# A matmul with a decayed running sum: what TensorE runs ahead of its first product

## The chip, the core and the metric

The kernel runs on one core of a Trainium2 chip. A core has a matrix engine (TensorE, PE in the profile, with its weight loads as PEld), three engines for elementwise work (VectorE or DVE, ScalarE or ACT, GpSimd or POOL), and SyncE (SP), which here only issues DMAs. Each engine has its own instruction queue, and they meet through semaphores. Work in on-chip memory lies in SBUF; products are written to PSUM. The metric is device time in microseconds, lower is better.

## The reference

```python
B, S, D = (16, 2048, 1024)          # x: B,S,D fp32; w: D,D; decay: D
xw = x @ w
out[:, 0, :] = xw[:, 0, :]
for t in range(1, S):
    out[:, t, :] = decay[None, :] * out[:, t - 1, :] + xw[:, t, :]
```

A matrix product of 32768 rows by 1024 by 1024, and along the 2048 time steps of each batch a first-order recurrence per column.

## The kernel before

Time is cut into 64 chunks of 512 steps, and two chunks make a group. The 1024 columns of the output are cut into 8 blocks of 128, whose columns stand on the partitions of PSUM, so that the recurrence runs along the free dimension. For a block and a chunk, TensorE sums over 8 slices `k` of 128 inputs: `wsb[:, k, n]` is the stationary operand, 512 time steps of the transposed x the moving one (`matmul`, L125 to L137, all recorded at L131). Both are bf16. The whole kernel is 4096 such products, some of them cut into smaller pieces at the start and the end.

Around them: GpSimd issues the loads of x (`load`, L105), one per quarter of the partitions, with the cast to bf16; VectorE transposes 32 by 32 blocks (`turn`, L115); ScalarE and VectorE sort even and odd inputs apart (`part`, L123) into `xt`. The products' first half takes `xw` as it is, the other `xt`. The recurrence runs on VectorE, either straight (L229) or in pairs of steps with help of ScalarE and GpSimd (L171, L191, L205, L210, L266); VectorE transposes back (L278), and SP issues the stores (L302). Weights come in through `load_w` (L319): one quarter of them, in four DMAs, on the queues of SP and ScalarE, the rest on GpSimd's; `settle` (L326) casts and sorts them into `wsb`.

The order on each engine is written out by hand: every instruction passes through `pin`, which keeps it in program order on its engine. `agenda` lists deeds by letter for each step; entry -99 is the start-up: `M` loads half a chunk, `U` a quarter of the weights, `w` and `W` settle weights on ScalarE and VectorE, `E` turns, `F` and `G` sort on VectorE and ScalarE, `K3` is `spin_on(3)`.

What the change touches is ahead of that. The zeroed tile `wide` (512 fp32 columns; `idle` is its bf16 view of 512 columns) and the zeroed `seed` feed five fp32 matmuls into a PSUM tile `spare` that nobody reads (`spin(5, seed, wide)`, L347, recorded at L345). They wait for the memsets and for a one-element copy on ScalarE (L338). Then `spin_on(3)` lets ScalarE copy one column of the fourth quarter of the first half chunk of x into `gate` (L361), and one bf16 matmul of `gate` with `idle` (L345) follows it; it too is not read. The first real product comes next.

Of the kernel before, what the change touches and what calls it, by code (L numbers as in the profile page):

```python
# [9 lines left out]
FP32 = mybir.dt.float32  # L10
BF16 = mybir.dt.bfloat16
# [3 lines left out]
def _ap(ap_obj: bass.AP, new_ap, extra_offset=0):  # L15
    return dataclasses.replace(
        ap_obj,
        ap=[list(p) for p in new_ap],
        offset=ap_obj.offset + extra_offset,
    )  # L20
# [5 lines left out]
def kernel(  # L26
# [26 lines left out]
    nc = tc.nc  # L53
    pin = tc.keep_in_program_order
# [15 lines left out]
    const = ctx.enter_context(tc.tile_pool(name="const", bufs=1))  # L70
# [5 lines left out]
    def ring(pool, name, count, shape, dtype=FP32):  # L76
        i = turns[name] = turns.get(name, -1) + 1
        return pool.tile(shape, dtype, name=f"{name}{i % count}")
# [238 lines left out]
    def load_w(queues, h, e):  # L317
        for i, q in enumerate((0, 2, 1, 3)):
            pin(queues[i % len(queues)].dma_start(  # L319
                out=stage[h, e][quad(q)].rearrange("p (m d) -> p m d", m=M),  # L320
                in_=_ap(w, [[2 * D, P], [2 * P * D, M], [1, CH]],
                        (q * CQ + e) * D + h * CH)))
# [6 lines left out]
    wide = const.tile([128, TL], FP32, name="wide")  # L329
    idle = wide[:, 0:TL // 2].bitcast(BF16)  # L330
    spare = ring(psp, "spare", 1, [128, TL])
    rows = const.tile([128, 2, P], FP32, name="rows")
    seed = const.tile([128, 128], FP32, name="seed")
    load_w((nc.sync, nc.scalar), 0, 0)
    pin(nc.vector.memset(wide, 0.0))
    pin(nc.vector.memset(rows, 0.0))
    pin(nc.vector.memset(seed, 0.0))
    pin(nc.scalar.copy(out=seed[:, 0:1], in_=wide[:, 0:1]))  # L338

    gate = const.tile([128, 128], BF16, name="gate")  # L340
    pin(nc.vector.memset(gate, 0.0))

    def spin(count, by, on):
        for _ in range(count):
            pin(nc.tensor.matmul(out=spare, lhsT=by, rhs=on, start=True, stop=True))  # L345

    spin(5, seed, wide)  # L347
    H = NJ // 2
    cuts = (((0, H + 2), (H + 2, NJ)), ((0, H), (H, NJ)))
    for q in range(NQ):  # L350
        pin(nc.sync.dma_start(
            out=rows[q * P:q * P + R],
            in_=_ap(decay, [[P, R], [CH, 2], [1, P]], q * CR)))
# [399 lines left out]
```

## Time and profile before

| | |
|---|---|
| time, median of 3 runs | 903.42 us (903.32 to 903.68) |
| time of the profiled execution | 903.94 us |
| span of the profile (first to last instruction) | 902.1 us |
| busy: PE, DVE, ACT, POOL | 889.2, 826.0, 685.2, 656.7 us |
| mean granted TensorE clock | 0.999 |
| first fp32 spin starts | 3.21 us |
| bf16 spin starts | 10.32 us |
| first product starts (L131) | 10.68 us |

The profile shows one execution. Times in it count from the span's start. A group of instructions is a line, an engine, an operation and its operands; behind the arrow in brackets stands what ended the idle time before it. A matmul's busy time runs to its modelled end, so that consecutive ones overlap and their starts tell the pace. An fp32 spin leaves two records of weight load and matmul.

### The profile page before, as it was taken

How to read it: one execution, taken by the hardware profiler on the slowest of the kernel's cores; microseconds unless marked ns; L12 is line 12 of the kernel's file. 1: busy time of each engine (PE TensorE's matmuls, PEld its weight loads, DVE VectorE, ACT ScalarE, POOL GpSimd, SP SyncE). 2: the span in 40 equal slices, each digit the busy share in tenths (PEclk: the TensorE clock that was granted, in tenths of full speed). 3: DMA queues.
4: the chain of work that ended last, by engine and by line, in shares of the span. 5: the costliest groups of instructions: out<-in, count | busy, mean ns of one | idle time of the engine just before them, and what ended most of it. 6: DMA issues, size and time to landing. Idle time of an engine off the chain costs nothing.

```text
span 902.1 us, 12228 instructions
## 1 busy us (share of the span) xinstructions
PE 889.2 (99%) x4130; PEld 412.4 (46%) x4211; DVE 826.0 (92%) x633; ACT 685.2 (76%) x957; POOL 656.7 (73%) x758
## 2 busy tenths in 40 slices
PE   8999999999999999999999999999999999999998
PEld 5544444444444444444444444444444444444444
DVE  4999989999999999999998999989999999999998
ACT  4888879777877877877778778777787787787743
POOL 7887778877767768677677677777777776876632
PEclk9999999999999999999999999999999999999999
DMA  9999999999999999999999999999999999999658
GB/s 190 190 208 250 236 209 215 215 238 248 241 260 254 247 266 249 242 238 233 216 245 219 228 235 220 236 220 231 238 227 222 226 240 223 233 220 211 187 140 234
DMA packets 403182, 204.77 MB, mean 227 GB/s; under 512 B 9392, under 2 KB 402096, under 8 KB 403120
## 3 DMA queue, kind: packets, MB, share of 16 engines
q0 software_dynamic: 137024, 68.70, 57.5%
q1 hardware_dynamic: 265808, 134.77, 57.1%
q8 instruction: 33, 0.54, 0.2%
q10 hardware_dynamic: 288, 0.52, 0.2%
q14 instruction: 29, 0.24, 0.1%
HBM read 138.42 MB, written 134.22 MB: 302 GB/s over the span
## 4 chain that ended last, share of the span: by engine, by line
PE 98%; DMA 1%; issue 1%; POOL 0%; DVE 0%; DVEq 0%; POOLq 0%
PE ps L131 96%; PE spare L131 1%; DMA ot<-in_w_dram 1%; POOL xb L105 0%; POOL ot L319 0%; PE spare L410 0%; PE ps L410 0%; DVE h L438 0%; DVE wsb L326 0%; DVEq L748 0%; DVEq L326 0%; POOLq L737 0%
## 5 line engine op out<-in xcount | busy, mean ns | idle before, releaser
L131 PE MATMUL ps<-xt,wsb 128*128 128x512 bf16 (+1 forms) x3959 | 861.7, 377 | 4.5 <-DVE wsb L326 0.3
L131 PEld LDWEIGHTS <-wsb 128*128 128x128 bf16 x4184 | 408.3, 98 | 477.4 <-DVE wsb L326 0.6
L205 POOL TENSOR_TENSOR xs<-h,xs 128x512 f32<-128x512 f32 (+1 forms) x190 | 242.5, 1277 | 184.7 <-ACT h L171 83.9
L191 ACT COPY xs<-ps 128x1024 f32<-128x1024 f32 (+1 forms) x190 | 188.7, 994 | 153.7 <-PE ps L131 143.0
L278 DVE STREAM_TRANSPOSE ot<-so 128x1024 f32<-128x1024 f32 (+2 forms) x264 | 300.6, 1176 | 3.0 <-POOL so L266 2.3
L266 POOL TENSOR_TENSOR so<-h,xs 128x512 f32<-128x512 f32 (+1 forms) x189 | 240.7, 1275 | 39.3 <-ACT h L171 27.3
L123 ACT COPY xt<-xw 128x2048 bf16<-128x2048 bf16 (+3 forms) x136 | 242.4, 1789 | 5.9 <-DVE xw L115 5.9
L105 POOL DMA_DIRECT2D xb<-in_x_dram x264 | 173.6, 659 | 8.0 <-DMA xb<-in_x_dram 5.4
L171 ACT ACTIVATE h<-so,dec 128x512 f32<-128x512 f32 (+1 forms) x189 | 144.8, 766 | 26.8 <-DVE so L210 23.4
L115 DVE STREAM_TRANSPOSE xw<-xb 128x2048 f32<-128x2048 f32 (+3 forms) x78 | 147.3, 1900 | 6.1 <-DMA xb<-in_x_dram 6.0
L210 DVE TENSOR_TENSOR_SCAN so<-spare,keep,xs 128x512 f32<-128x512 f32 (+1 forms) x97 | 119.9, 1240 | 27.4 <-POOL xs L205 26.8
L210 DVE TENSOR_TENSOR_SCAN so<-spare,xs 128x512 f32<-128x512 f32 x93 | 113.3, 1220 | 25.8 <-POOL xs L205 22.6
L171 ACT ACTIVATE h<-ps,dec 128x512 f32<-128x512 f32 (+1 forms) x190 | 129.7, 684 | 0.0
L229 DVE TENSOR_TENSOR_SCAN so<-dec,ps 128x1024 f32<-128x1024 f32 x34 | 76.9, 2262 | 1.1 <-ACT h L171 0.6
L229 DVE TENSOR_TENSOR_SCAN so<-dec,keep,ps 128x1024 f32<-128x1024 f32 (+2 forms) x35 | 75.5, 2156 | 0.8 <-PE ps L131 0.8
L270 ACT COPY keep<-so 128x1 f32<-128x1 f32 x136 | 25.3, 189 | 9.3 <-DVE so L229 8.7
L201 ACT COPY so<-keep 128x1 f32<-128x1 f32 x97 | 18.4, 192 | 3.6 <-DVE ot L278 3.5
L199 POOL MEMSET so<- 128x1 f32 x93 | 10.6, 116 | 2.7 <-DVE ot L278 2.7
L131 PE MATMUL spare<-xt,wsb 128*128 128x512 bf16 (+3 forms) x60 | 12.6, 330 | 0.0
L131 PE MATMUL ps<-xw,wsb 128*128 128x256 bf16 (+3 forms) x72 | 12.2, 306 | 0.0
L345 PE MATMUL spare<-wide,seed 128*128 128x512 f32 x10 | 6.1, 772 | 3.2 <-ACT seed L338 3.2
L319 POOL DMA_DIRECT2D ot<-in_w_dram x12 | 6.5, 544 | 0.9 <-DMA xb<-in_x_dram 0.3
(43 smaller groups left out, 37.1 us busy)
## 6 DMA issues: line engine op xcount, KB each, us to landing
out_dram<-ot SPq DMA_DIRECT2D x236, 512.0 KB, 9.3
xb<-in_x_dram POOLq DMA_DIRECT2D x248, 256.0 KB, 7.6
out_dram<-ot SPq DMA_DIRECT2D x56, 128.0 KB, 2.2
out_dram<-ot SPq DMA_DIRECT2D x8, 256.0 KB, 4.9
ot<-in_w_dram POOLq DMA_DIRECT2D x12, 128.0 KB, 5.5
xb<-in_x_dram POOLq DMA_DIRECT2D x8, 128.0 KB, 4.5
out_dram<-xb SPq DMA_DIRECT2D x3, 256.0 KB
xb<-in_x_dram POOLq DMA_DIRECT2D x4, 160.0 KB, 6.3
```

What stands on the lines that cost most here:

```text
L105: pin(nc.gpsimd.dma_start(out=xb_of[c][quad(q), j0:j1], in_=_ap(x, [[D, P], [P * D, j1 - j0], [1, CQ]], (b * S + t0 + j0 * P) * D + q * CQ)))
L115: pin(nc.vector.transpose(out=dst.rearrange("p (m j i) -> p j m i", m=M, i=P)[:, j0:j1, m0:m1], in_=src.rearrange("p (j m c) -> p j m c", ...
L123: pin(copy(out=xt_of[c][:, m0:m1, :, j0 * P:j1 * P], in_=src))
L131: return pin(nc.tensor.matmul(out=ps[:, t0 % ps.shape[1]:][:, 0:t1 - t0], lhsT=lhs, rhs=rhs, start=(k == 0 and t0 == start), stop=(k == K ...
L171: pin(nc.scalar.activation(out=h[:, i * size:(i + 1) * size], in_=src, func=mybir.ActivationFunctionType.Copy, scale=dec[:, self.n:self.n ...
L191: pin(nc.scalar.copy(out=self.xs[:, i * size:(i + 1) * size], in_=ps))
L205: pin(nc.gpsimd.tensor_tensor(out=odds, in0=self.g, in1=odds, op=ALU.add))
L210: pin(nc.vector.tensor_tensor_scan(out=so[:, 3:T + 2:2], data0=squares[-1][:, n:n + 1].to_broadcast([128, T // 2]), data1=self.xs[:, 1:T:2 ...
L229: return pin(nc.vector.tensor_tensor_scan(out=so[:, t + 2:t + 2 + size], data0=dec[:, n:n + 1].to_broadcast([128, size]), data1=ps, initia ...
L266: pin(nc.gpsimd.tensor_tensor(out=self.so[:, 2:T + 2:2], in0=self.h, in1=self.xs[:, 0:T:2], op=ALU.add))
L270: pin(nc.scalar.copy(out=self.keep, in_=self.so[:, self.T + 1:self.T + 2]))
L278: pin(nc.vector.transpose(out=outlet.ot[:, :, c0:c0 + P], in_=self.so[:, 2 + t0:2 + t0 + nj * P].rearrange("p (i t) -> p i t", t=P)))
```

## The change

The five fp32 spins go, and with them `seed`, its memset and the one-element copy on ScalarE. In their place one weight load of `gate` (zeroed now at the very start) is followed by 28 bf16 matmuls of `gate` with `idle`, 512 columns each, that don't load weights of their own. A weight load and matmuls that rely on it must not be parted, so they stand in a section that the scheduler treats as a unit. The memset of `gate` moves ahead, that of `rows` behind the first weight loads of `w`. `spin_on`, the agenda and all that follows are as before.

```diff
-    seed = const.tile([128, 128], FP32, name="seed")
+    gate = const.tile([128, 128], BF16, name="gate")
+    pin(nc.vector.memset(wide, 0.0))
+    pin(nc.vector.memset(gate, 0.0))
+
+    def stream(out, lhsT, rhs, start, stop):
+        te = nc.tensor
+        return te.add_instruction(mybir.InstMatmult(
+            name=nc.get_next_instruction_name(),
+            ins=[te.lower_ap(rhs), te.lower_ap(lhsT)],
+            outs=[te.lower_ap(out)],
+            start_tensor_calc=start,
+            stop_tensor_calc=stop,
+            ldweights=False,
+            tile_size=(128, 128),
+            tile_position=(0, 0),
+        ))
+
+    with tc.tile_critical():
+        nc.tensor.ldweights(gate)
+        for _ in range(28):
+            stream(spare, gate, idle, True, True)
     load_w((nc.sync, nc.scalar), 0, 0)
-    pin(nc.vector.memset(wide, 0.0))
     pin(nc.vector.memset(rows, 0.0))
-    pin(nc.vector.memset(seed, 0.0))
-    pin(nc.scalar.copy(out=seed[:, 0:1], in_=wide[:, 0:1]))
-
-    gate = const.tile([128, 128], BF16, name="gate")
-    pin(nc.vector.memset(gate, 0.0))
...
-    spin(5, seed, wide)
```

Built, the section becomes a block of TensorE's program of its own, between two jumps; the other engines jump past it. The scheduler sets that place behind the first DMA of each queue: one w load on ScalarE, one on SP, one x load on GpSimd. The instructions of each engine around it, with their waits:

```
TensorE   no-op          waits for the memsets of wide and gate
          semaphore      waits for ScalarE's first w load and GpSimd's first x load
          semaphore      waits for SP's first w load
          jump           waits for the memset of rows
          weight load of gate, 28 matmuls, jump
          drain          waits for the section
          no-op          signals that the drain is done
          weight load of gate (spin_on), waits for ScalarE's copy; one bf16 matmul; the products
ScalarE   w load, jump, w load, table load, two casts of w (wait for the four w loads),
          copy into gate: waits for the fourth x load and for TensorE's drain
          copies of xt (L123), ...
SP        w load, jump, w load, four loads of decay
GpSimd    x load, jump, three x loads, four w loads, x loads
VectorE   memsets of wide, gate and rows, jump, two casts of w, transposes
```

Before, the table load stood behind ScalarE's two w loads and ahead of the seed copy.

## The prediction

> **What bounds the kernel now.** I read the chain of waits first, to see which engine sets the end, then the list of TensorE's waits, then the first 14 us of the timeline engine by engine, and last the end of the chain.
>
> The chain that ended last by engine, three of its longest pieces (start us, us, what), and then all that TensorE waited for (us in total, times, longest):
>
> ```profile
> PE 98%; DMA 1%; issue 1%; POOL 0%; DVE 0%; DVEq 0%; POOLq 0%
> ```
>
> ```profile
> 25.86 10.74 PE ps L131 x49
> 47.64 10.74 PE ps L131 x49
> 58.44 10.96 PE ps L131 x50
> ```
>
> ```profile
> PE spare L345 <- ACT seed L338: 3.2, 1, 3.2
> PE spare L345 <- ACT gate L361: 1.0, 1, 1.0
> PE ps L131 <- DVE wsb L326: 0.3, 1, 0.3
> ```
>
> From the first product on, TensorE is the chain. A steady piece gives 10.74 / 49 = 0.219 us for a 512-column product, the end of the last one included. After the last wait in the list, at 13 us, TensorE waits for nobody to the end; so what delays the first product delays the end, less what can be taken back from that one wait.
>
> Now the start: TensorE's products, its weight loads, ScalarE, GpSimd and VectorE (start us, us, engine, line, operation, idle time before it).
>
> ```profile
> 3.21 6.12 PE L345 MATMUL spare<-wide,seed 128*128 128x512 f32 x10 [3.21 <-ACT seed L338]
> 10.32 0.39 PE L345 MATMUL spare<-wide,gate 128*128 128x512 bf16 x1 [0.98 <-ACT gate L361]
> 10.68 0.59 PE L131 MATMUL ps<-xw,wsb 128*128 128x320 bf16 x3
> ...
> 13.39 0.58 PE L131 MATMUL ps<-xt,wsb 128*128 128x320 bf16 x3 [0.30 <-DVE wsb L326]
> ```
>
> ```profile
> 5.08 0.34 PEld L345 LDWEIGHTS spare<-wide,seed 128*128 128x128 f32 x1 [0.52 <-issue]
> 5.94 0.34 PEld L345 LDWEIGHTS spare<-wide,seed 128*128 128x128 f32 x1 [0.52 <-issue]
> 6.60 0.19 PEld L345 LDWEIGHTS spare<-wide,seed 128*128 128x128 f32 x1 [0.32 <-issue]
> 7.03 0.19 PEld L345 LDWEIGHTS spare<-wide,seed 128*128 128x128 f32 x1 [0.24 <-issue]
> ```
>
> ```profile
> 6.55 1.14 ACT L326 CAST wsb<-ot 128x512 bf16<-128x512 f32 x2 [3.39 <-DMA ot<-in_w_dram]
> 10.07 0.19 ACT L361 COPY gate<-xb 32x1 bf16<-32x1 bf16 x1 [2.39 <-DMA xb<-in_x_dram]
> 10.66 1.98 ACT L123 COPY xt<-xw 128x640 bf16<-128x640 bf16 x3 [0.40 <-DVE xw L115]
> ```
>
> ```profile
> 7.72 0.57 POOL L105 DMA_DIRECT2D xb<-in_x_dram  x1 [1.75 <-DMA xb<-in_x_dram]
> ...
> 10.28 0.56 POOL L105 DMA_DIRECT2D xb<-in_x_dram  x1 [0.34 <-DMA xb<-in_x_dram]
> ```
>
> The reader is to see three things. The spins run from 3.21 to 9.33 and are over before the data is there. TensorE's cold and warm clock can be read off the weight loads: 5.94 - 5.08 = 0.86 us between halves of an fp32 spin early, 7.03 - 6.60 = 0.43 later; the step 5.94 to 6.60 (0.66) is 0.46 us at the slow pace and the rest at the fast one, so the clock rose at about 6.4, 3.2 us after the first spin. (The granted clock reads 1.00 throughout, so it does not show this.) And the fourth quarter of x landed at 10.0: that released the gate copy (10.07), the one bf16 spin (10.32) and the first product (10.68).
>
> **Where the new spins begin.** They are atomic for the scheduler, and the built order shows the price. On TensorE, ahead of the jump into the section, stand waits for the last writes that the program had issued till then: the first w load on ScalarE's queue, the first w load on SP's, the first x load on GpSimd's, and the memsets. In the kernel before, the spins waited for a memset and a one-element copy alone (3.21). The first w loads are in by 6.55 (the casts above need all four). The first x load released GpSimd's fifth x load at 7.72; the same kind of release for the fourth quarter shows 10.28 on GpSimd, but the copy on ScalarE could go after its semaphore at 10.0, so GpSimd sees it some 0.27 late. Landing: 7.72 - 0.27 = 7.45. This load is still GpSimd's first work and goes out at 1.32 as before. Two semaphore instructions and a jump on the sequencer: semaphore instructions measure 0.017 to 0.05, the weight load 0.10; say 0.25 in all. First stream at 7.7.
>
> The jump itself has no row. Below it can't be under 0; above, the nearest row is GpSimd's 0.87 us between its last start-up memset and its first DMA, which holds a jump and a barrier. That memset ends at 0.45, and SP and ScalarE, past the same barrier and a jump of their own, issue their first DMA at 0.75: 0.3 for both together, so I take the low end. On SP, ScalarE and GpSimd a jump now stands between the first and the second load of the queue, at the same price; the loads behind it would have to be 5 us late to be felt beside the delay found below.
>
> **How long they run.** A bf16 stream of 512 columns: half of the weight-load step, 0.43 cold and 0.215 warm (the steady 0.219 agrees). With 3.2 us cold: 3.2 / 0.43 = 7.4 streams; 20.6 x 0.215 = 4.4 us more; 7.6 together, to 15.3. Bounds: no cold phase at all, 28 x 0.215 = 6.0 (1.6 less); twice 3.2 cold, 14.9 streams, then 13.1 x 0.215, 9.2 (1.6 more). The seed was zeros too, so I take the row's 3.2.
>
> The Trainium skill (TensorE: Matmul & The Clock Gate, Part 1) has the clock rise about 4 us into sustained activity, in a window that runs freely and so can fall anywhere; the trace's 3.2 is a little quicker. With 4 us the sum would be 0.4 us longer.
>
> **From the last stream to the first product.** The section ends in a drain on TensorE, and in the built order ScalarE's gate copy (L361 of the page) now waits for that drain, because the copy writes the weights that the streams read. Steps: last results leave 0.39 - 0.215 = 0.17 after the stream's last column (the 0.39 row); drain, no-op and ScalarE's semaphore, three hops of 0.05 (ScalarE's seed copy ended at 3.16 and TensorE went at 3.21), plus 0.07 ahead of ScalarE's start (10.0 to 10.07); the copy 0.19; a hop 0.05; the gate's weight load and bf16 spin, 0.23. Sum 0.17 + 0.15 + 0.07 + 0.19 + 0.05 + 0.23 = 0.86. First product at 15.3 + 0.86 = 16.15, against 10.68: 5.5 late.
>
> **What is queued behind.** ScalarE's queue stands still behind the gate copy until 15.7: the three copies of L123 (1.98), one weight copy (0.62), then nine more. TensorE takes 16 products of 320 columns first (10.68 to 12.93 before, 2.25 us), that is until 18.4, and needs the weight copy by the fifth product of the second set, 18.4 + 4 x 0.14 = 18.95; ScalarE has it at 15.7 + 1.98 + 0.62 = 18.3. It fits by 0.6; if the cover went, each 0.1 there would cost 0.1. VectorE's and GpSimd's start-up work doesn't depend on TensorE and is simply done earlier against it, so the stall before 13.39 goes: 13.39 - 12.93 = 0.46 back. What else is added costs nothing on the path: the table load that sat at 1.68 (1.28 us) now stands before the casts, 6.5 to 7.8, and moves them to end at 9.0; TensorE needs these weights at 16. Without the late start this cover would still hold, as 9.0 is before 10.0. The removed memset (0.17) and seed copy (0.19) were hidden behind loads.
>
> After that TensorE has no idle time to give up: the delay stays to the end. Sum: 5.5 - 0.5 = **5.0 us later**. The profiled span of 902.1 becomes 907.1; that execution took 903.94, 1.8 around the span and 0.5 over the median of the three runs. On the median, 903.42 + 5.0 = 908.4.
>
> **Rivals.**
>
> *The clock rises a window later.* Same start; up to 9.2 instead of 7.6 us of streams, +6.6: 910.0. For it: the only rise in the trace is one sample, and nothing ties it to the kernel's start. Against: the cost counts in halves, since streams run on meanwhile. The page named above speaks for it, as a free-running window could delay the rise by up to another window.
>
> *The jumps cost code loading.* One exposed jump at the upper bound 0.87, the one behind the streams being fetched while they run: +5.9, 909.3. Against: the start-up jumps on SP and ScalarE show little. The Trainium skill (Runtime: NRT & Kernel Launch, Instruction fetch mechanics) says a taken jump out of the fetched pages stalls for a load; the target here lies close by, and no row of this kernel shows such a stall.
>
> *Not slower: the entry waits don't bind.* If the streams start when the memsets are done (1.70), they end at 1.8 + 7.6 = 9.4, drained by 9.7, and the gate copy still goes at 10.07: change 0, 903.4. It decides at a start of 10.0 - 0.3 - 7.6 = 2.1 us: earlier starts are free, later ones cost one for one. For it: the streams' own operands need memsets alone. Against: the waits for the loads stand in the built order, and x can't land at 2.1 when it is issued at 1.32 and takes 6 us.
>
> *Faster.* It would need x to land sooner than 10.0 or the 0.46 stall to go with no delay: at most 0.5, under what can be told apart.
>
> **How the numbers follow.** The forecast 0.74, the late clock 0.14, code loading 0.07, no effect 0.04, faster 0.01. Predicted 908.4. Range: below, a shorter cold phase or an earlier landing, 1.2 less: 907.2; above, the late clock with a part of the jump: 910.4. A measurement of this kernel can tell 0.2% (1.8 us) from no change; only the no-effect and the faster case lie within that. A saving larger than that is in none of the cases, and I leave it 0.01: faster 0.01, same 0.05, slower 0.94.
>
> **What would show it.** In the profile after: the first bf16 stream at 7.7, released by the x load; the last one ending near 15.3; a step in the streams' spacing from 0.43 to 0.215 some 3.2 us in; the gate copy at 15.6 instead of 10.07; the first L131 product near 16.15; no wait of L131 for wsb; steady pieces unchanged at 0.219. Streams starting before 2.1 would prove it wrong, as would a first product at 16 with an end that is not late, for then TensorE was not the chain.

## The result

The changed kernel takes 909.12 us (908.05 to 909.48, 3 runs) against 903.42: slower by 5.7 us, ratio 1.006, 95% interval 1.0037 to 1.0083. In a second set of runs it took 909.10 (908.56 to 909.28, 4 runs) against 903.36, ratio 1.0061 (1.0046 to 1.0076). The prediction was 908.4, with 907.2 to 910.4 as its range.

The profiled execution took 909.48, its span 907.7 (902.1 before). First the chain that ended last, by engine, and then all waits of TensorE (us in total, times, longest), both of the changed kernel:

```profile
PE 98%; DVE 0%; DVEq 0%; ACT 0%; issue 0%; ACTq 0%
```

```profile
PE spare L339 <- DVE wsb L326: 7.7, 1, 7.7
PE spare L359 <- ACT gate L374: 0.5, 1, 0.5
```

TensorE is still the chain, and the wait of L131 for weights is gone from the list. The releaser in the first row is a guess of the profile: VectorE's cast at 6.75 is merely the last event that it could place there; by the built order TensorE stood at a wait for the first loads. The start on the timeline, first TensorE, then ScalarE and GpSimd (start us, us, engine, line, operation, idle time before and its releaser):

```profile
7.67 8.25 PE L339 MATMUL spare<-wide,gate 128*128 128x512 bf16 x28 [7.67 <-DVE wsb L326]
16.39 0.39 PE L359 MATMUL spare<-wide,gate 128*128 128x512 bf16 x1 [0.46 <-ACT gate L374]
16.61 0.59 PE L131 MATMUL ps<-xw,wsb 128*128 128x320 bf16 x3
...
18.87 0.57 PE L131 MATMUL ps<-xt,wsb 128*128 128x320 bf16 x3
```

```profile
6.71 1.28 ACT L326 ACT_TABLE_LOAD   x1 [6.71 <-DMA ot<-in_w_dram]
...
16.14 0.19 ACT L374 COPY gate<-xb 32x1 bf16<-32x1 bf16 x1 [7.01 <-PEq L350]
16.36 1.98 ACT L123 COPY xt<-xw 128x640 bf16<-128x640 bf16 x3
18.24 0.61 ACT L326 COPY wsb<-ot 128x512 bf16<-128x512 bf16 x1
```

```profile
7.52 1.23 POOL L105 DMA_DIRECT2D xb<-in_x_dram  x2 [1.56 <-DMA xb<-in_x_dram]
```

The streams occupy 7.67 to 15.92, and the first product starts at 16.61 instead of 10.68, 5.93 later. The second set of products follows the first without the gap of before (18.87, where 13.39 had a wait ahead of it): 0.46 back. That leaves 5.47 at the second set, and the piece of VectorE that follows TensorE's last one in the chain starts 5.43 later. Of the two chains, the changed kernel's first and then that of before (start us, us, what):

```profile
903.27 0.56 DVE h L451
```

```profile
897.84 0.56 DVE h L438
```

What is lost at the start arrives at the end unchanged. The last stores add 0.2.

At the entry TensorE's queue shows what it did (operation, count, shortest/median/longest in ns, first and last start in us):

```profile
L761 PEldq EVENT_SEMAPHORE  x2: 51/1334/2617, 4.7 to 7.3; - x2
L761 PEldq COMPARE_BRANCH  x1: 179/179/179, 7.4 to 7.4; - x1
```

The first semaphore instruction was held for 2.62 us and let go at 7.3. It waits for ScalarE's first w load and GpSimd's first x load, and the x load came last: ScalarE's table load, released by w, went at 6.71, while GpSimd, which waits for the same x load, went on at 7.52. The jump took 0.18. At the other end:

```profile
L350 PEldq DRAIN  x1: 8033/8033/8033, 7.9 to 7.9; - x1
```

The drain stood from 7.9 to 15.9, and ScalarE's gate copy started 0.2 after it.

### The profile page after: what moved, and what is told of

Its sections match the earlier page's. It is cut to its first block, busy times and chain, and to the rows that moved or that the text cites. A ratio compares the mean times of both kernels' runs of the same rounds, so it can differ in the third digit from the quotient of the medians.

```text
span 907.7 us, 12324 instructions
## 1 busy us (share of the span) xinstructions
PE 895.2 (99%) x4229; PEld 410.1 (45%) x4202; DVE 825.9 (91%) x632; ACT 684.8 (75%) x956; POOL 657.0 (72%) x758
## 4 chain that ended last, share of the span: by engine, by line
PE 98%; DVE 0%; DVEq 0%; ACT 0%; issue 0%; ACTq 0%
PE ps L131 96%; PE spare L131 1%; PE spare L423 0%; PE ps L423 0%; DVE h L451 0%; PE spare L359 0%; DVEq L761 0%; ACT gate L374 0%; ACTq L374 0%
## 5 line engine op out<-in xcount | busy, mean ns | idle before, releaser
L131 PE MATMUL ps<-xt,wsb 128*128 128x512 bf16 (+2 forms) x4040 | 865.9, 377 | 0.0
L131 PEld LDWEIGHTS <-wsb 128*128 128x128 bf16 x4184 | 408.4, 98 | 476.7
L339 PE MATMUL spare<-wide,gate 128*128 128x512 bf16 x28 | 8.3, 466 | 7.7 <-DVE wsb L326 7.7
L131 PE MATMUL spare<-xt,wsb 128*128 128x512 bf16 (+3 forms) x60 | 12.6, 329 | 0.0
L131 PE MATMUL ps<-xw,wsb 128*128 128x256 bf16 (+3 forms) x72 | 12.2, 306 | 0.0
```

What stands on the lines that cost most here:

```text
L131: return pin(nc.tensor.matmul(out=ps[:, t0 % ps.shape[1]:][:, 0:t1 - t0], lhsT=lhs, rhs=rhs, start=(k == 0 and t0 == start), stop=(k == K ...
```

## The experiments

All times are medians, and ratios stand against the kernel before on the same chip. The starts in the table, and the lines shown, are those of one profiled execution each.

| kernel | streams start | first product | time | ratio, 95% |
|---|---|---|---|---|
| before | (3.21) | 10.68 | 903.4 | 1 |
| changed, again | 7.69 | 16.43 | 909.10 | 1.0046 to 1.0076 |
| 28 spins, no section | 1.54 | 10.49 | 903.11 | 0.9988 to 1.0007 |
| no spins | none | 10.81 | 904.63 | 1.0004 to 1.0023 |
| section, 1 stream | 8.31 | 10.81 | 904.91 | 1.0008 to 1.0027 |
| section ahead of the loads | 1.98 | 11.67 | 904.19 | 1.0001 to 1.0020 |
| section, 14 streams | 8.70 | 14.91 | 906.46 | 1.0022 to 1.0048 |
| section, second gate | 8.23 | 17.62 | 909.72 | 1.0046 to 1.0080 |
| spins, then section | 10.16 | 18.83 | 910.86 | 1.0063 to 1.0093 |

**The same 28 spins without the section.**

```diff
-    with tc.tile_critical():
-        nc.tensor.ldweights(gate)
-        for _ in range(28):
-            stream(spare, gate, idle, True, True)
...
+    spin(28, gate, idle)
```

> The 28 bf16 spins of the changed kernel as ordinary matmuls, each with its own weight load, and no section. Theory (the section's entry waits for loads are the cause): the spins start with the memsets, at 1.6, end near 9.4, the gate copy goes at 10.1, the first product at 10.7 and the stall of 0.46 before the second set of products is back: 903.4, within 0.4 of before. Rival (28 streams are too many whatever starts them): the first product stays near 16, 908 to 909.

Measured 903.11, no difference from before. Its TensorE:

```profile
1.54 8.44 PE L355 MATMUL spare<-wide,gate 128*128 128x512 bf16 x28 [1.54 <-DVE gate L335]
10.26 0.39 PE L355 MATMUL spare<-wide,gate 128*128 128x512 bf16 x1 [0.28 <-ACT gate L371]
10.49 0.59 PE L131 MATMUL ps<-xw,wsb 128*128 128x320 bf16 x3
```

```profile
10.02 0.19 ACT L371 COPY gate<-xb 32x1 bf16<-32x1 bf16 x1 [0.71 <-PE spare L355]
```

```profile
9.88 1.69 DVE L115 STREAM_TRANSPOSE xw<-xb 128x320 f32<-128x320 f32 x4 [2.20 <-DMA xb<-in_x_dram]
```

The spins wait for the memset alone and are over at 9.98, which is 0.6 later than expected, as their cold phase lasted 4.5 us (worked out below). The copy of x into `gate` was released by the last of them, by the profile, and went 0.14 behind VectorE's first transpose of x; before it went 0.05 ahead of it (10.07 and 10.12). So 28 spins from 1.54 on held the copy by some 0.2 here: they just fit, and the time shows no loss. Neither the number of streams alone nor bf16 is the cause, and a weight load for each stream costs nothing that shows: the 28 take 8.44 us here against 8.25 and 8.05 with one shared load, but single records start 0.427 (cold) and 0.216 us (warm) apart in all three, and only the cold phase is longer here (4.5 us against 4.1 and 3.7).

**No spins at all.** The section is deleted, and nothing takes its place.

> No spins and no section; only the one bf16 spin that waits for x is left. Theory: nothing holds the first product, which starts at 10.7, but on a cold clock: about 3.2 to 3.8 us of products at half pace, 1.6 to 1.9 us lost, up to 0.46 of it regained from the stall before the second set: 904.6 to 905.3. It also says what the five fp32 spins are worth. Rival (the clock doesn't matter here): 903.4.

Measured 904.63, at the low end of what was expected. The first product is on time, but slow:

```profile
10.81 1.01 PE L131 MATMUL ps<-xw,wsb 128*128 128x320 bf16 x3
11.62 0.47 PE L131 MATMUL spare<-xw,wsb 128*128 128x320 bf16 x1
11.88 1.00 PE L131 MATMUL ps<-xw,wsb 128*128 128x320 bf16 x3
```

In the kernel before, the fifth product starts here:

```profile
11.25 0.58 PE L131 MATMUL ps<-xw,wsb 128*128 128x320 bf16 x3
```

Four products take 11.88 - 10.81 = 1.07 us where the kernel before takes 11.25 - 10.68 = 0.57. So the five fp32 spins ahead of the first product are worth 904.63 - 903.40 = 1.2 us to the kernel. The change warms the clock too, and loses 5.7 us doing it.

**The section with one stream.**

```diff
-        for _ in range(28):
+        for _ in range(1):
```

> The section kept, with one stream in place of 28. Theory: the stream starts at 7.7 as in the changed kernel, the drain is over by 8.6, before x has landed at 10.0, so the section costs nothing and the run is like the one without spins, with a cold clock: 904.6 to 905.3, first product at 10.7. Rival (jumps, drain and the held queues are what costs): 1 us or more above the run without spins, up to 908.

Measured 904.91, in the expected range and 0.3 over the kernel without spins, with overlapping intervals.

```profile
8.31 0.61 PE L339 MATMUL spare<-wide,gate 128*128 128x512 bf16 x1 [8.31 <-DVE wsb L326]
10.41 0.61 PE L359 MATMUL spare<-wide,gate 128*128 128x512 bf16 x1 [1.50 <-ACT gate L374]
10.81 1.01 PE L131 MATMUL ps<-xw,wsb 128*128 128x320 bf16 x3
```

TensorE waits at the entry as in the changed kernel, passes both jumps and the drain, and stands again from 8.92 to 10.41, waiting for x. Jumps, drain and held queues are covered; only streams that outlast the landing of x at 10 are paid for.

**The section ahead of the loads.** Small memsets into the targets of the first loads, placed behind those of `wide`, `gate` and `rows` on VectorE, hold the loads back until the scheduler has set the section.

```diff
+    xb_of[0] = ring(sb, "xb", 3, [128, NJ, CQ], BF16)
     with tc.tile_critical():
...
+    pin(nc.vector.memset(rows, 0.0))
+    pin(nc.vector.memset(xb_of[0][:, 0, 0:1], 0.0))
+    pin(nc.vector.memset(room[0][:, 0:1], 0.0))
     load_w((nc.sync, nc.scalar), 0, 0)
-    pin(nc.vector.memset(rows, 0.0))
```

> The section with its 28 streams, but the first loads of w and x are made to wait for small memsets of their targets, so that no load has been issued ahead of the section and its entry waits for memsets alone. Price of the edit: x is issued at about 1.75 instead of 1.31, the first w loads at 1.8 instead of 0.75. Theory: streams from 1.9 to 9.6, first product with x at 11.0 to 11.4, so 903.6 to 904.3. Rival (the section itself, or 28 streams, cost 5 us): 908 to 909.

Measured 904.19, in the expected range.

```profile
1.98 9.05 PE L339 MATMUL spare<-wide,gate 128*128 128x512 bf16 x28 [1.98 <-DVE ot L357]
11.45 0.39 PE L362 MATMUL spare<-wide,gate 128*128 128x512 bf16 x1 [0.41 <-ACT gate L377]
11.67 0.59 PE L131 MATMUL ps<-xw,wsb 128*128 128x320 bf16 x3
```

```profile
11.20 0.19 ACT L377 COPY gate<-xb 32x1 bf16<-32x1 bf16 x1 [0.55 <-PEq L351]
```

```profile
11.03 1.69 DVE L115 STREAM_TRANSPOSE xw<-xb 128x320 f32<-128x320 f32 x4 [2.00 <-DMA xb<-in_x_dram]
```

Section, shared weight load, 28 streams, drain and the copy's wait for it are all still there; taking the loads out of the entry wait, at the price of issuing them 0.5 to 0.9 later, gives back 4.9 of the 5.7 us. This is the experiment that settles the cause. Two steps inside it were off: the streams ended at 11.03 and not at 9.6, as their cold phase lasted 5.8 us (worked out below), and the copy, with x in by 11.03, waited for the drain until 11.20. So the first product came at 11.67, later than the expected 11.0 to 11.4.

**Fourteen streams.** `range(14)` in place of `range(28)`.

> The section with 14 streams in place of 28. Theory: same start at 7.7, the 14 streams that go are warm ones of 0.216, 3.0 us: last stream ends at 12.5, first product 13.6, 905.4 to 906.2. Rival (the section costs a fixed 5 us): 908 to 909.

Measured 906.46, a little above the expected 905.4 to 906.2.

```profile
8.70 5.52 PE L339 MATMUL spare<-wide,gate 128*128 128x512 bf16 x14 [8.70 <-DVE wsb L326]
14.91 0.59 PE L131 MATMUL ps<-xw,wsb 128*128 128x320 bf16 x3
```

In the profiled execution (907.18) the section began 1.0 late, because the loads landed late in it: GpSimd's fifth x load went at 8.55, ScalarE's table load, which waits for w, at 7.81 (6.71 in the changed kernel). Measured from the start of the streams, the first product comes after 6.21 us, against 8.94 and 8.74 with 28 streams in the two profiles of the changed kernel: 2.5 to 2.7 for fourteen streams, near the 3.0 of fourteen warm ones. The cold phase was longer here, 4.7 us against 4.1 and 3.7 (worked out below), which costs 0.3 and 0.5 and makes up the rest. There is no fixed 5 us.

**Weights of its own for the spin that waits for x.**

```diff
+    mark = const.tile([128, 128], BF16, name="mark")
+    pin(nc.vector.memset(mark, 0.0))
...
-        pin(nc.scalar.copy(out=gate[quad(q), 0:1], in_=xb_of[0][quad(q), 0, 0:1]))
-        spin(1, gate, idle)
+        pin(nc.scalar.copy(out=mark[quad(q), 0:1], in_=xb_of[0][quad(q), 0, 0:1]))
+        spin(1, mark, idle)
```

> The spin that waits for x gets weights of its own, so that ScalarE's copy no longer waits for the drain of the 28 streams. Theory: the copy goes at 10.1 and ScalarE's start-up work with it; TensorE is held by the streams alone, and of the 1.1 us from the last stream to the first product some 0.3 goes: first product near 16.2 to 16.3, 0.3 below the changed kernel. Rival (holding ScalarE's queue is what costs): back to 904 to 905.

Measured 909.72: no gain in time, where 0.3 was expected. TensorE and ScalarE:

```profile
8.23 8.99 PE L341 MATMUL spare<-wide,gate 128*128 128x512 bf16 x28 [8.23 <-DVE wsb L326]
17.41 0.38 PE L361 MATMUL spare<-wide,mark 128*128 128x512 bf16 x1 [0.19 <-PEq L352]
17.62 0.58 PE L131 MATMUL ps<-xw,wsb 128*128 128x320 bf16 x3
```

```profile
10.35 0.19 ACT L376 COPY mark<-xb 32x1 bf16<-32x1 bf16 x1 [0.57 <-DMA xb<-in_x_dram]
```

The copy is free, at 10.35, and from the end of the last stream's record to the first product there are 17.62 - 17.22 = 0.40 us instead of 16.61 - 15.92 = 0.69: the 0.3 that was expected. But this execution began its streams 0.56 later and ran them 0.74 longer (8.99 against 8.25), which hides it; 0.3 is under what the runs tell apart. The holding of ScalarE's queue is excluded as the cause.

**Spins first, then the section.** Sixteen ordinary bf16 spins ahead of it, to have the streams run on a warm clock.

```diff
+    for _ in range(16):
+        pin(nc.tensor.matmul(out=spare, lhsT=gate, rhs=idle, start=True, stop=True))
     with tc.tile_critical():
```

> 16 ordinary bf16 spins from 1.6 on, then the section with its 28 streams. The scheduler now sets the section later, behind all four w loads and three of the four x loads, and its entry waits for these. Theory: the section starts when the third quarter of x has landed, 9.0 to 9.2, and the streams run warm, 28 x 0.216 = 6.0 (unless the idle time from 7 to 9 cools the clock: 7.9): end 15.2, first product near 16.2, so the time of the changed kernel, 908 to 909, from a start 1.5 us later. Rival (the start of the section doesn't follow the loads): streams begin at 7 and the first product comes at 14, 906.5.

Measured 910.86, above both expectations.

```profile
1.54 6.22 PE L351 MATMUL spare<-wide,gate 128*128 128x512 bf16 x16 [1.54 <-DVE gate L335]
10.16 7.90 PE L339 MATMUL spare<-wide,gate 128*128 128x512 bf16 x28 [2.40 <-DMA xb<-in_x_dram]
```

Stretches of the same kernel (from:to, length, TensorE's busy time with its instructions, granted clock, DMA share, GB/s):

```profile
6.50:7.50 1.00, 1.00 (x5) 1.00 1.43 183
...
11.00:12.00 1.00, 1.00 (x4) 0.50 1.25 196
12.00:13.00 1.00, 1.00 (x4) 0.50 1.44 192
13.00:14.00 1.00, 1.00 (x4) 0.68 1.43 190
14.00:15.00 1.00, 1.00 (x6) 1.00 1.43 191
```

What stood on TensorE's queue at the section's entry (operation, count, shortest/median/longest in ns, first and last start in us):

```profile
L763 PEldq EVENT_SEMAPHORE  x5: 51/51/51, 9.4 to 9.8; - x5
L763 PEldq COMPARE_BRANCH  x1: 179/179/179, 9.9 to 9.9; - x1
```

The section did move with its waits. It follows the third quarter of x: the last of the waits let go at 9.4 (GpSimd, released by the same quarter, went on at 9.61), and five semaphore instructions and the jump, 0.75 together, made that 10.16. They are most of the difference to the expected 9.0 to 9.2. But the streams ran cold again: after the spins TensorE was idle for 2.40 us, and the granted clock fell to 0.50 until somewhere between 13 and 14. A warm-up that ends 2.4 us early is lost here; idle time of 1.0 (before) and 0.5 (changed) did not do that.

**The changed kernel again.**

> The changed kernel once more, on the same chip as the next three and with more runs. Theory: 908.4 to 909.2; its runs spread by about 1 us or more, since the time at which the clock rises after the streams' start differs from run to run and now lies on the path, where the kernel before hides it (its runs lie within a few tenths). Rival (the spread is the chip's): the runs of before spread as far.

The median, 909.10, is in the range. The expected spread did not show: 908.56 to 909.28 in 4 runs, against 903.02 to 904.34, which is wider, in 8 runs of before. With the first 3 runs of the changed kernel at 908.05 to 909.48, the spread doesn't decide. The kernel without the section has the narrowest, 902.90 to 903.29 in 10 runs. That the spread of the changed kernel's runs comes from its exposed clock and loads is therefore not shown by the times; the profiles show that both terms vary, as told below.

No version beat both kernels: the one without the section ties with before.

## Why the prediction was right, step by step

*TensorE sets the end, and a late first product arrives at the end.* Right: 5.47 late at the second set of products, 5.43 at the end of TensorE's part of the chain.

*Where the streams begin.* Predicted 7.7, measured 7.67 and 7.69 in the changed kernel. The landing was 7.3, not 7.45, and the way from it to the first stream 0.4, not 0.25: two small errors that cancel. In other executions of the same entry the start was 8.23, 8.31 and 8.70, up to 1.0 later, so that the figure came out so close is luck. The wait itself was right. In all five profiles with this entry, GpSimd's fifth x load, which waits for the first, went at 7.52, 7.54, 8.07, 8.15 and 8.55, and the streams at 7.67, 7.69, 8.23, 8.31 and 8.70, 0.15 to 0.16 behind it each time; ScalarE's table load, which waits for w, went 0.85 to 1.07 ahead of them. The x load is the wait that ends last.

*How long they run.* This is the term that was mis-sized: 7.6 predicted. The last stream starts at 15.92 - 0.38 = 15.54, and its last column is in at 15.54 + 0.22 = 15.76: 8.1 us. The pace, from two stretches of the changed kernel's streams:

```profile
L339 PE MATMUL spare<-wide,gate x8: 609/634/634, 7.7 to 10.6; 128*128 128x512 bf16 x8
```

```profile
L339 PE MATMUL spare<-wide,gate x14: 379/379/379, 12.7 to 15.6; 128*128 128x512 bf16 x14
```

Seven steps from 7.7 to 10.6 are 0.42 each and thirteen from 12.7 to 15.6 are 0.22, so both paces were right (the starts of single records in this trace lie 0.427 and 0.216 apart). The share was not: with n cold streams, 0.427 n + 0.216 (28 - n) = 8.1 gives n = 9.7, 4.1 us of cold clock where I took 3.2 from the one rise in the trace of before. The Trainium skill (TensorE: Matmul & The Clock Gate, Part 1) puts the rise about 4 us into activity and lets it vary by 500 ns with a free-running window; the 4.1 and 3.7 us in the two profiles of the changed kernel agree with that better than with the single row that I preferred, while over all the runs here the phase spread further, from 3.2 to 5.8 us. I held a clock that rises later for a rival of its own, with 0.14; the 4.1 us measured lie inside that spread, so a phase longer than 3.2 was no separate case but the ordinary variation of the sum's own term. A cold phase of 5.6 or 5.8 us, as in two other executions, would have added about 0.8 us more.

*From the last stream to the first product.* Predicted 0.86, measured 16.61 - 15.76 = 0.85; the experiment with a second gate took 0.3 of it away.

*What is queued behind.* Right: the stall of 0.46 went, and ScalarE's weight copy was done at 18.85, 0.56 before the fifth product of the second set (18.87 + 4 x 0.135 = 19.41). The table load at 6.71 cost nothing.

*The rivals.* Code loading at the jumps fell: the jump at the entry took 0.18, and with one stream the section costs 0.3 in the medians, within the intervals. The Trainium skill's stall for a taken jump out of the fetched pages (Runtime: NRT & Kernel Launch, Instruction fetch mechanics) shows nowhere here. That the entry waits don't bind fell too: the streams started at 7.67. An early start was nearly free once those waits were taken away: with a start at 1.98 the streams were done at 11.03, by when x, issued later there, was in, and the time was 904.19.

The step from 5.0 to the 5.47 at the second set of products is thus 0.5 from the clock; the last 0.2, at the end of the stores, had no place in the sum.

## What to carry to other kernels

In these builds a section that the scheduler treats as one unit waits, at its entry, for what was issued before it on the other queues, and not only for what its own instructions read. Look at the built order for the waits ahead of its jump before reckoning with it as filler: here the filler's own operands were ready at 1.5 us, and it started at 7.7. Work that only warms a clock should end shortly before the real work (1.0 us of idle time kept the clock here, 2.4 us lost it), and cost less than the 1.2 us that it saves.

## What the runs showed of the hardware

The cold phase differs from execution to execution. Worked out as above from the streams' records (their span less 0.16, the end of the last one), it was 4.1 and 3.7 us in the two profiles of the changed kernel, 4.7 with fourteen streams, 5.6 with the second gate, 5.8 with the section ahead of the loads, 4.5 with the 28 spins and no section, and 5.3 in the 16 spins ahead of the section; 3.4 after the idle time of 2.4 us, and 3.2 in the kernel before. What sets it in an execution is not shown.

The granted clock of the profile reads 1.00 in the cold start of every one of these kernels, though products take twice as long there; it showed 0.50 only where a clock that had been warm fell again. Pace at a start is to be read from starts of instructions, not from that column.

A semaphore instruction whose wait is already met still takes its place on TensorE's queue: five of them and a jump made 0.75 us.
